# A gated state-space layer on one core: eight groups' scans rearranged around their small matrix products

## The chip, the core and the metric

The kernel runs on one core of a Trainium2 chip. The core has a matrix engine, TensorE (PE in the profile; PEld is its loading of weights), and three engines for elementwise work: VectorE (DVE), ScalarE (ACT) and GpSimd (POOL). SyncE (SP) issues the DMA transfers. Each engine takes its instructions in order and waits on semaphores where it needs another's result. PE writes to PSUM, eight banks of 512 float32 columns by 128 partitions; all other operands lie in SBUF. The metric is the time of one execution on the device in microseconds, the median of several runs.

## The reference

One layer of a hybrid decoder, for a prompt of 256 positions with 16 learned ones ahead of it, and for 8 samples of 8 positions each: 336 rows of 2048 channels.

```python
h = rms_norm(x, norm_w)
proj = h @ w_in
z, xbc, dt_raw, sc_b, sc_c, sc_h, sc_z, g_a, g_b = split_proj(proj)
...
xbc = jax.nn.silu(xbc_c + ssd_conv_b)
...
y_diag = jnp.einsum('bcijgr,bcjgrp->bcigrp', wts, xc)
...
chunk_states = jnp.einsum('bcjgr,bcjgrp,bcjgn->bcgrpn', to_end, xc, bc)
...
y_off = jnp.einsum('bcign,bcgrpn->bcigrp', cc, h_in) * jnp.exp(acum)[..., None]
...
y = gated_group_rms_norm(y.reshape(bsz, length, D_INNER), z, ssd_norm_w)
y_a = y @ w_ssd_out
...
merged = jax.nn.sigmoid(g_a) * y_a + jax.nn.sigmoid(g_b) * y_b
return x + merged @ w_o, conv_new, state, sconv_new
```

The scan is over chunks: within a chunk the outputs are weighted sums (`y_diag`), a state of 64 x 128 per head is carried from chunk to chunk, and what it contributes is `y_off`. The eight samples start from states of their own, which are inputs, and return new ones. The 64 heads fall into 8 groups of 8.

## The kernel before

All matrix products of the big weights are made in a split form: each float32 weight block is read by one DMA into `wraw`, ACT makes a rounded part `whi` (L86), DVE the rest `wlo` (L88), and PE multiplies `whi` with both parts of the activations (L94, L95) and `wlo` with the first (L98). A block is 128 x 1024; each of the three buffers has three copies. The type fp32r of these parts goes through PE in one instruction per product, a plain float32 product in two.

After a first stage (short convolution, gates, tables of the decay) comes the stage that the change touches: a loop over the 8 groups. For each group, four kinds of units follow one another, and each is a stretch of big products: `z_units` (4 units, the gate z of this group), `out_units` (8 units, the output projection of the group before, into `ya`), in the first and the last group `gate_units`, and `conv_units` (6 units, the inputs of the next group). Between the units the scan of the group, the generator `ssd`, is woven in: it is cut into steps by `yield`, and `weave` takes steps out so that 23 are done by the end of the units. Instructions of a step on PE, DVE and ACT are held behind the last L98, L88 and L86 traced before them; those of POOL and SP are not held. A planner orders what is free to move.

The steps, by their lines in `ssd`: `rows(c)` transposes a chunk's inputs and forms its products (two ms tiles); `decay` and `weights` make the matrices of weights W on DVE, ACT and POOL; `carry(c)` scales the state on POOL; `state(c)` (L496) forms a chunk's contribution to the state on PE in an ms tile and adds it, on DVE (L500), or copies it, on ACT, for the first chunk (L502). In the step of `state(1)` stand the carried outputs of the samples, `po` (L535 to L539): eight products with 32 columns of weights, four of them side by side in the array. One step later DVE takes them into `yo` (L543), and the shrinks (L506) begin: eight POOL instructions, two a step over four steps, which multiply the samples' states in place by their decay. Two steps after that come the weighted sums `yb` (L549 to L556), 32 float32 products on 64-column tiles, then four transposes of `yo` (L559) and the sums on DVE (L561 to L564). The states and inputs of the last chunk, which holds the meta positions and the samples, are split into parts and written to DRAM (L576, L577), read back in another order (L584 to L592), and used in `state(2)` with 64 rows (L604) and in the samples' states `up` with 32 rows (L610), added on DVE (L613). The gated result is squared on ACT (L581), summed over tiles on POOL (L594) and over channels on PE (L599); the factor r (L600 to L602) is spread over all partitions by a product of ones with a diagonal (L616 to L620).

PSUM holds two `pj` tiles (big products, one bank each), two `ms` tiles (one bank each) and one `yb` tile of four banks. `pj` is given back when the last reader has read it: for z these are ACT's tanh (L431) and DVE's product (L432).

Of the kernel before, what the change touches and what calls it, by code (L numbers as in the profile page):

```python
# [7 lines left out]
F32 = mybir.dt.float32  # L8
# [5 lines left out]
P = 128  # L14
# [20 lines left out]
def fb(ap):  # L35
    return ap.bitcast(F32)


def bc(ap, shape):
    return ap.to_broadcast(shape)  # L40
# [3 lines left out]
def tile_hybrid_step(ctx, tc, xT, w1, w2, wdt, wso, wsc, wo, cmask, vec, hvec, convst, sconvst, h0T,  # L44
# [330 lines left out]
    with tc.tile_pool(name="pb", bufs=2) as pb:  # L375
# [48 lines left out]
        def z_units(g, st):  # L424
            st["zs"] = []
            for t in range(4):
                pz = proj(w1[4 * g + t], META)
                z = pb.tile([P, TV + 4], F32, name="zs", bufs=4)
                if t == 0:
                    nc.gpsimd.memset(z[:, TV:], 0.0)  # L430
                nc.scalar.activation(z[:, :TV], pz, AF.Tanh, scale=0.5)  # L431
                nc.vector.scalar_tensor_tensor(z[:, :TV], z[:, :TV], 1.0, pz, add, mult)  # L432
                st["zs"].append(z)
                yield

# [6 lines left out]
        def ssd(g, st):  # L442
# [39 lines left out]
            def weights(c):  # L482
                n, m, w = CH[c][1], NT[c], W[c]
                nc.vector.tensor_tensor(w[:n], w[:n], bc(cbm[c][:n, :m].unsqueeze(1), [n, 8, m]), mult)
                xe[c] = big("xe", 2)
                nc.gpsimd.tensor_tensor(split(xe[c][:n]), split(xdt[c][:n]), bc(hv(tet[:n, c, :], g), [n, 8, HP]), mult)
                if c == 1:
                    nc.gpsimd.tensor_tensor(E, E, bc(CT[:, P:P + PX].unsqueeze(1), [P, 8, PX]), mult)

            def carry(c):  # L490
                hst[c] = hn = big("hst", 2)
                if c:
                    nc.gpsimd.tensor_tensor(split(hn), split(hst[c - 1]), bc(hv(cdec[:, c - 1, :], g), [P, 8, HP]),
                                            mult)

            def state(c, lhs, rhs):  # L496
                pst = ps.tile([P, 512], F32, name="ms")
                nc.tensor.matmul(pst, lhs, rhs, start=True, stop=True)  # L498
                if c:
                    nc.vector.tensor_tensor(hst[c], hst[c], pst, add)  # L500
                else:
                    nc.scalar.activation(hst[c], pst, AF.Copy)  # L502

            def shrink(b0, b1):
                for b in range(b0, b1):
                    nc.gpsimd.tensor_tensor(split(h0[b]), split(h0[b]), bc(hv(decS[:, b, :], g), [P, 8, HP]), mult)  # L506
# [25 lines left out]
            decay(2)  # L532
            yield
            state(1, bt[1], xe[1])
            po = ps.tile([P, 512], F32, name="ms")  # L535
            for s_ in range(2):
                for q in range(4):
                    nc.tensor.matmul(po[32 * q:32 * q + 32], CZ[:, 64 * q + 32 * s_:64 * q + 32 * s_ + 32],  # L538
                                     h0[2 * q + s_], start=s_ == 0, stop=s_ == 1)  # L539
            yield  # L540
            weights(2)
            yo = big("xe", 2)
            nc.vector.tensor_tensor(split(yo), split(po), bc(hv(eaY, g), [P, 8, HP]), mult)  # L543
            shrink(0, 2)
            yield
            carry(2)
            shrink(2, 4)
            yield
            yb = ps.tile([P, 4, 512], F32, name="yb", bufs=1)  # L549
            for t in range(4):  # L550
                for i, (x, w, t0, n) in enumerate(((xdt[0], W[0], 0, P), (xdt[1], W[1], P, PX), (hst[0], E, P, PX),
# [17 lines left out]
            nc.scalar.activation(bhh[:80, 0, :], bt[2][:80], AF.Copy)  # L569
            nc.vector.tensor_tensor(xe2[:80, 1, :], xe[2][:80], fb(xe2[:80, 0, :]), sub)  # L570
            nc.vector.tensor_tensor(bhh[:80, 1, :], bt[2][:80], fb(bhh[:80, 0, :]), sub)
            shrink(4, 6)
            yield
            xq, bq = xq_d[g % 2], bq_d[g % 2]
            for r in range(2):
# [3 lines left out]
            for t in range(4):  # L579
                nc.vector.tensor_tensor(ys[:, t, META:], ys[:, t, META:], zs[t][:, :TV], mult)  # L580
                nc.scalar.activation(zs[t][:, :TV], ys[:, t, META:], AF.Square)  # L581
            shrink(6, 8)
            yield
            x3 = big("xdt", 3, F32R)  # L584
            b3 = pb.tile([P, P], F32R, name="b3", bufs=1)
            xh = pb.tile([P, 2, 576], F32R, name="xh", tag="W")[:, :, :512]
            bh = pb.tile([P, 2, P], F32R, name="bh", bufs=1)
            for d, q in ((x3, xq), (b3, bq)):
                nc.sync.dma_start(fb(d[:64]), q[:16].rearrange("p r c -> (p r) c"))
            for d, q in ((xh, xq), (bh, bq)):  # L590
                for u in range(2):
                    nc.sync.dma_start(fb(d[:, u, :]), q[16 + 32 * u:48 + 32 * u].rearrange("p r c -> (p r) c"))  # L592
            for t in range(1, 4):
                nc.gpsimd.tensor_tensor(zs[0][:, :TV], zs[0][:, :TV], zs[t][:, :TV], add)  # L594
            yield
# [4 lines left out]
            r = pb.tile([107, 3], F32, name="rs_r", bufs=1)  # L600
            nc.vector.tensor_scalar(r, pr[:107, 0:3], 1.0 / 512, 4.0 * EPS, mult, add)
            nc.gpsimd.tensor_tensor(r, r, bc(mhalf[:107], [107, 3]), ALU.pow)  # L602
            yield
            state(2, b3[:64], x3[:64])  # L604
            nc.sync.dma_start(ssmp[g], hst[2])
            for u in range(2):
                up = ps.tile([P, 4, 512], F32, name="yb", bufs=1)
# [5 lines left out]
                    nc.vector.tensor_tensor(h, h, up[:, 2 * b:2 * b + 2, :], add)  # L613
                yield
                if u == 0:
                    dg = big("xe", 2)[:107, :321]  # L616
                    nc.vector.tensor_tensor(eights(dg, 107), bc(ident[:107, :107].unsqueeze(1), [107, 3, 107]),
                                            bc(r.unsqueeze(2), [107, 3, 107]), mult)
                    rs = ps.tile([P, 512], F32, name="ms")
                    nc.tensor.matmul(rs[:, :321], ones[:107, :], dg, start=True, stop=True)  # L620
                for b in range(2):
                    nc.sync.dma_start(ssms[g, :, 4 * u + 2 * b:4 * u + 2 * b + 2, :], h0t[2 * u + b])
                yield
# [237 lines left out]
```

## Time and profile before

| what | us |
|---|---|
| median of 3 runs | 1869.42 |
| lowest and highest | 1868.22, 1871.44 |
| the profiled execution, its own time | 1870.82 |
| its span | 1868.7 |
| DVE: weight rests L88, 480 of them | 604.2 busy, 1259 ns each |
| POOL: shrinks L506, 64 of them | 72.4 busy, 1167 ns each |
| DVE: samples' states L613, 32 of them | 38.7 busy, 1214 ns each |
| ACT: z's tanh L431, 32 of them | 13.8 busy, 431 ns each |
| DVE: z's product L432, 32 of them | 15.4 busy, 480 ns each |

How to read the views: a page gives the busy time of each engine, the span in 40 slices with the busy share of each in tenths, the chain of work that ended last, and groups of instructions by line, with the idle time before them and what ended it. A timeline has start and duration in us, engine, line, operation, output and inputs, the shape (for PE the rows and columns of the array in use, then rows and columns of the moving operand), and how many were merged. PE's products overlap, so a row's duration is longer than the distance to the next one's start; what a product costs PE is that distance. Each float32 product appears as two instructions. Times shown by the chain of waits are from the same execution. The granted clock of PE was full in nearly the whole span (mean 0.996).

### The profile page before, as it was taken

Reading aid. Unit: us, or ns where it says so; the run is one execution under the profiler, and the core shown is the slowest. Engines: PE = TensorE matmul, PEld = TensorE weight load, DVE = VectorE, ACT = ScalarE, POOL = GpSimd, SP = SyncE. Lnnn points to the kernel's source line nnn. Section 1 sums busy time; section 2 is a strip of 40 time slices with the busy share of each in tenths; the row PEclk is TensorE's granted clock in tenths of the full one; section 3 lists DMA queues with packets and bytes.
Section 4 is the critical chain, followed back from the end, with each engine's and each line's share of the span. In section 5 each row is a group of like instructions: output and inputs, shape, how many; then the busy total and the mean of one; then the engine's idle time right before and its main releaser. Section 6 shows DMA issues by size and latency. Waiting matters only on the chain.

```text
span 1868.7 us, 31432 instructions
## 1 busy us (share of the span) xinstructions
PE 1836.0 (98%) x12618; PEld 1792.8 (96%) x12618; DVE 1122.9 (60%) x1746; ACT 748.8 (40%) x1038; POOL 299.5 (16%) x395
## 2 busy tenths in 40 slices
PE   7999999999999999999999999999999999999996
PEld 7999999999999999999899999999999999999996
DVE  6844444454533335657577677876867677674533
ACT  6433333333333334445454353544435345333431
POOL 0100000000000001132221412214132231300011
PEclk9999999999999999999999999999999999999998
DMA  6444444444444446456466574655756466575553
GB/s 221 145 151 147 147 153 151 149 147 151 153 158 157 154 165 224 148 186 226 149 215 204 176 236 150 216 193 175 246 154 227 165 197 224 162 260 169 172 172 108
DMA packets 117185, 331.73 MB, mean 178 GB/s; under 512 B 12464, under 2 KB 38704, under 8 KB 117040
## 3 DMA queue, kind: packets, MB, share of 16 engines
q1 hardware_dynamic: 117040, 329.73, 53.9%
q8 instruction: 99, 1.62, 0.3%
q14 instruction: 46, 0.38, 0.1%
HBM read 296.80 MB, written 32.88 MB: 176 GB/s over the span
## 4 chain that ended last, share of the span: by engine, by line
PE 49%; DVE 1%; issue 1%; DMA 0%; ACT 0%; POOLq 0%; POOL 0%; DVEq 0%; ACTq 0%
PE pj L94 15%; PE pj L95 15%; PE pj L98 15%; PE yb L555 1%; PE ms L498 1%; PE ms L538 1%; DVE wlo L88 0%; PE ms L462 0%; DVE ya L754 0%; PE yb L610 0%; PE ms L559 0%; PE ms L465 0%; PE ms L620 0%; DMA wraw<-wso 0%; PE ms L599 0%
## 5 line engine op out<-in xcount | busy, mean ns | idle before, releaser
L88 DVE TENSOR_TENSOR wlo<-wraw,whi 128x1024 fp32r<-128x1024 f32 x480 | 604.2, 1259 | 490.6 <-ACT whi L86 244.4
L94 PE MATMUL pj<-hhi,whi 128*128 128x320 f32 (+3 forms) x2944 | 888.5, 313 | 0.0
L95 PE MATMUL pj<-hlo,whi 128*128 128x320 f32 (+3 forms) x2944 | 882.3, 312 | 0.0
L86 ACT ACTIVATE whi<-wraw 128x1024 fp32r<-128x1024 f32 x480 | 508.4, 1059 | 891.5 <-PE pj L95 753.9
L94 PEld LDWEIGHTS pj<-hhi,whi 128*128 128x128 f32 x2944 | 553.7, 188 | 5.4 <-issue 2.8
L95 PEld LDWEIGHTS pj<-hlo,whi 128*128 128x128 f32 x2944 | 553.0, 188 | 0.7
L98 PE MATMUL pj<-hhi,wlo 128*128 128x320 f32 (+3 forms) x2944 | 498.3, 311 | 0.0
L98 PEld LDWEIGHTS pj<-hhi,wlo 128*128 128x128 f32 x2944 | 453.2, 188 | 0.0
L94 PE MATMUL pj<-yh,whi 128*128 128x320 f32 x512 | 154.9, 314 | 4.3 <-DVE zs L432 2.5
L95 PE MATMUL pj<-yl,whi 128*128 128x320 f32 x512 | 152.7, 310 | 0.0
L94 PEld LDWEIGHTS pj<-yh,whi 128*128 128x128 f32 x512 | 96.0, 188 | 13.0 <-issue 6.4
L95 PEld LDWEIGHTS pj<-yl,whi 128*128 128x128 f32 x512 | 96.1, 188 | 0.0
L98 PE MATMUL pj<-yh,wlo 128*128 128x320 f32 x512 | 95.8, 308 | 0.0
L398 DVE SCALAR_TENSOR_TENSOR cacc<-pad,V,cacc 128x360 f32<-128x360 f32 (+1 forms) x144 | 89.6, 622 | 2.8
L647 DVE TENSOR_TENSOR ya<-ya,pj 128x320 f32<-128x320 f32 x112 | 54.1, 485 | 60.0 <-PE pj L98 59.5
L506 POOL TENSOR_TENSOR h<-h,decS 128x512 f32<-128x512 f32 x64 | 72.4, 1167 | 108.4 <-PE ms L538 94.4
L98 PEld LDWEIGHTS pj<-yh,wlo 128*128 128x128 f32 x512 | 80.3, 188 | 0.0
L197 POOL COPY SCS<-up 128x2 f32<-128x2 f32 x16 | 19.4, 1214 | 369.7 <-DVE up L191 366.7
L95 PE MATMUL pj<-vlo,whi 128*128 128x320 f32 x256 | 75.5, 309 | 0.0
L94 PE MATMUL pj<-vhi,whi 128*128 128x320 f32 x256 | 75.5, 309 | 0.0
L392 POOL COPY cs<-pad 128x3 f32<-128x3 f32 x48 | 42.4, 884 | 124.4 <-ACT pad L389 124.4
L95 PEld LDWEIGHTS pj<-vlo,whi 128*128 128x128 f32 x256 | 48.1, 188 | 0.0
(219 smaller groups left out, 1428.5 us busy)
## 6 DMA issues: line engine op xcount, KB each, us to landing
wraw<-w SPq DMA_DIRECT2D x352, 512.0 KB, 3.9
wraw<-wso SPq DMA_DIRECT2D x64, 512.0 KB, 3.5
wraw<-wsc SPq DMA_DIRECT2D x32, 512.0 KB, 3.8
h<-h0T SPq DMA_DIRECT2D x32, 512.0 KB, 5.7
ssms<-h SPq DMA_DIRECT2D x32, 512.0 KB, 5.7
wraw<-wo SPq DMA_DIRECT2D x32, 512.0 KB, 3.8
xq_d<-xe SPq DMA_DIRECT2D x16, 320.0 KB, 3.7
W<-ac_d SPq DMA_DIRECT2D x8, 576.0 KB, 6.7
```

Source lines behind the costliest of these rows:

```text
L86: latest["act"] = nc.scalar.activation(hi[:, :n], raw[:, :n], AF.Copy).ins
L88: latest["dve"] = nc.vector.tensor_tensor(lo[:, :n], raw[:, :n], fb(hi[:, :n]), sub).ins
L94: nc.tensor.matmul(out, w, xh(k0 + k), start=first and k == 0, stop=False)
L95: nc.tensor.matmul(out, w, xl(k0 + k), start=False, stop=False)
L98: latest["pe"] = nc.tensor.matmul(out, w, xh(k0 + k), start=False, stop=last and k == nk - 1).ins
L197: nc.gpsimd.tensor_copy(SCS[:, j, 0, :], up[:, 256:258])
L392: nc.gpsimd.tensor_copy(cs[:, 0, :], pad[:, 272:275])
L398: nc.vector.scalar_tensor_tensor(acc[:, i0:], pad[:, i0 + k:360 + k], col(V_CW, 4 * j + k), acc[:, i0:], mult, add)
L498: nc.tensor.matmul(pst, lhs, rhs, start=True, stop=True)
L506: nc.gpsimd.tensor_tensor(split(h0[b]), split(h0[b]), bc(hv(decS[:, b, :], g), [P, 8, HP]), mult)
L538: nc.tensor.matmul(po[32 * q:32 * q + 32], CZ[:, 64 * q + 32 * s_:64 * q + 32 * s_ + 32], h0[2 * q + s_], start=s_ == 0, stop=s_ == 1)
L647: nc.vector.tensor_tensor(ya[:, m, :TV], ya[:, m, :TV], pp[:, :TV], add)
```

## The change

Five edits in the scan and in `z_units`:

1. z: the tanh goes to a tile of its own (`cth`, one buffer, shared with the convolution); ACT also copies z out of `pj`, and DVE's product reads the two from SBUF.
2. `state(0)` and `state(1)` use the first bank of the `yb` tile instead of an `ms` tile.
3. The carried outputs `po` and `yo` move from the steps after `state(1)` into the step of the weighted sums, directly ahead of them; the shrinks move behind that step, three, three and two in the next three steps.
4. The prompt's last state multiplies all 128 rows; two POOL memsets clear rows 64 to 127 of its two operands.
5. The factor r is split into two fp32r parts on DVE, and spread by two fp32r products of 320 columns instead of one float32 product of 321.

```diff
@@ z_units
-                nc.scalar.activation(z[:, :TV], pz, AF.Tanh, scale=0.5)
-                nc.vector.scalar_tensor_tensor(z[:, :TV], z[:, :TV], 1.0, pz, add, mult)
+                th = pb.tile([P, 360], F32, name="cth", bufs=1)[:, :TV]
+                nc.scalar.activation(th, pz, AF.Tanh, scale=0.5)
+                nc.scalar.activation(z[:, :TV], pz, AF.Copy)
+                nc.vector.scalar_tensor_tensor(z[:, :TV], th, 1.0, z[:, :TV], add, mult)
@@ state
-                pst = ps.tile([P, 512], F32, name="ms")
+                pst = ps.tile([P, 512], F32, name="ms") if c == 2 else ps.tile([P, 4, 512], F32, name="yb", bufs=1)[:, 0]
@@ ssd, after state(1)
             state(1, bt[1], xe[1])
+            yield
+            weights(2)
+            yield
+            carry(2)
+            yield
             po = ps.tile([P, 512], F32, name="ms")
...
-            yield
-            weights(2)
             yo = big("xe", 2)
             nc.vector.tensor_tensor(split(yo), split(po), bc(hv(eaY, g), [P, 8, HP]), mult)
-            shrink(0, 2)
-            yield
-            carry(2)
-            shrink(2, 4)
-            yield
             yb = ps.tile([P, 4, 512], F32, name="yb", bufs=1)
@@ the next three steps
-            shrink(4, 6)
+            shrink(0, 3)
...
-            shrink(6, 8)
+            shrink(3, 6)
...
+            for d in (x3, b3):
+                nc.gpsimd.memset(fb(d[64:]), 0.0)
             for d, q in ((x3, xq), (b3, bq)):
                 nc.sync.dma_start(fb(d[:64]), q[:16].rearrange("p r c -> (p r) c"))
...
+            shrink(6, 8)
@@ after r
+            rh = pb.tile([107, 2, 3], F32R, name="rs_h", bufs=1)
+            nc.vector.tensor_copy(rh[:, 0, :], r)
+            nc.vector.tensor_tensor(rh[:, 1, :], r, fb(rh[:, 0, :]), sub)
...
-            state(2, b3[:64], x3[:64])
+            state(2, b3, x3)
@@ factor
-                    dg = big("xe", 2)[:107, :321]
-                    nc.vector.tensor_tensor(eights(dg, 107), bc(ident[:107, :107].unsqueeze(1), [107, 3, 107]),
-                                            bc(r.unsqueeze(2), [107, 3, 107]), mult)
                     rs = ps.tile([P, 512], F32, name="ms")
-                    nc.tensor.matmul(rs[:, :321], ones[:107, :], dg, start=True, stop=True)
+                    for i in range(2):
+                        dg = big("xe", 2, F32R)[:107, :321]
+                        nc.vector.tensor_tensor(eights(dg, 107), bc(ident[:107, :107].unsqueeze(1), [107, 3, 107]),
+                                                bc(fb(rh[:, i, :]).unsqueeze(2), [107, 3, 107]), mult)
+                        nc.tensor.matmul(rs[:, :TV], onesR[:107, :], dg[:, :TV], start=i == 0, stop=i == 1)
```

## The prediction

> **What bounds the kernel now.** I read the page first: the busy shares, the slices and the chain of work that ended last.
>
> ```profile
> span 1868.7 us, 31432 instructions
> ...
> PE 1836.0 (98%) x12618; PEld 1792.8 (96%) x12618; DVE 1122.9 (60%) x1746; ACT 748.8 (40%) x1038; POOL 299.5 (16%) x395
> ...
> PE   7999999999999999999999999999999999999996
> ...
> PE 49%; DVE 1%; issue 1%; DMA 0%; ACT 0%; POOLq 0%; POOL 0%; DVEq 0%; ACTq 0%
> ...
> L86 ACT ACTIVATE whi<-wraw 128x1024 fp32r<-128x1024 f32 x480 | 508.4, 1059 | 891.5 <-PE pj L95 753.9
> ```
>
> PE is busy in every slice and the chain names hardly anything else. The last row says that the engines that feed it are ahead: ACT stood idle 891.5 us before its weight conversions, 753.9 of them until PE gave a buffer back. So work added on ACT, DVE or POOL costs nothing until it uses up that lead; a saving must be PE time, either a wait of PE or an instruction on PE. The view of PE's waits lists the first kind, the chain in order of time shows how often the second comes.
>
> ```profile
> PE pj L94 <- DVE zs L432: 2.5, 3, 1.4
> PE ms L464 <- ACT hst L502: 1.6, 1, 1.6
> ```
>
> ```profile
> 1030.80 1.85 PE ms L538 x16
> ...
> 1145.44 1.85 PE ms L538 x16
> ```
>
> The scan of one group of heads comes round every 114.6 us, eight times in all. I work out one middle group (its state products of the samples, L538, at 1030.8) and multiply by eight.
>
> **The last state on all rows (L604).** PE's timeline in the two steps that add the samples' states: the first step also holds the prompt's last state (L498, 64 rows), the second doesn't.
>
> ```profile
> 1076.10 1.40 PE L98 MATMUL pj<-hhi,wlo 128*128 128x336 f32 x8
> 1077.43 0.50 PE L498 MATMUL ms<-xdt,b 64*128 64x512 f32 x1
> 1077.86 0.51 PE L610 MATMUL yb<-xh,bh 32*128 32x512 f32 x4
> ...
> 1078.56 0.32 PE L95 MATMUL pj<-hlo,whi 128*128 128x336 f32 x1
> ...
> 1092.55 1.40 PE L98 MATMUL pj<-hhi,wlo 128*128 128x336 f32 x8
> 1093.88 0.51 PE L610 MATMUL yb<-xh,bh 32*128 32x512 f32 x4
> ...
> 1094.57 0.31 PE L95 MATMUL pj<-hlo,whi 128*128 128x320 f32 x1
> ```
>
> From the L98 row to the L95 row it is 2.46 us with L498 and 2.02 without, so the 64-row product takes 0.44 us of PE. The same product over the whole array should cost what its columns cost. The rows of the next step give that price:
>
> ```profile
> 1084.59 1.40 PE L98 MATMUL pj<-hhi,wlo 128*128 128x336 f32 x8
> 1085.83 0.70 PE L620 MATMUL ms<-xe,CR 107*128 107x321 f32 x2
> ...
> 1086.52 0.32 PE L95 MATMUL pj<-hlo,whi 128*128 128x336 f32 x1
> ```
>
> Eight full-array products of 336 columns take 1.24 us, 0.155 each; 512 columns make 0.236. The step from the full array to the 32-row products stays, and is in the 2.02 already. Saved: 0.44 - 0.236 = 0.20, times eight **1.6 us** (1.4 to 1.8). The two memsets that fill rows 64 to 127 are POOL's; I bound each by one shrink (1.13 us, below) and cost them at nothing, since L498 comes some 30 us after the last reader of that buffer. If SP's load of the lower rows had to wait for the memset, the weight loads behind it on SP would wait too, on a lead of about two blocks.
>
> **The factor in two parts (L616 to L620).** By the same rows, from L620 to the L95 after it are 0.69 us, less one ordinary 0.155: 0.535 us for a float32 product of 321 columns, which runs as two instructions. The new form is two fp32r products of 320 columns, 0.148 each by the row above, 0.295 together. Saved 0.24, times eight **1.9 us** (1.5 to 2.1). What DVE gets instead:
>
> ```profile
> 1075.52 0.49 DVE L617 TENSOR_TENSOR xe<-CR,rs_r 107x321 f32<-107x321 f32 x1
> ```
>
> That is one more diagonal of 0.49 us and two tiny splits, each below that: under 1.5 us per group. DVE had the diagonal ready at 1076.0, PE used it at 1085.83; the cover is ten us, and what would be late without it is L620 itself, by at most the 1.5. The second diagonal takes the buffer of yo, whose last reader is L559, long done.
>
> **The carried outputs beside the weighted sums (L535 to L543 moved behind carry(2)).** Rows of the two places that become one, and DVE's evacuation from the listing of groups by shape:
>
> ```profile
> 1029.78 1.02 PE L498 MATMUL ms<-xe,bt 128*128 128x512 f32 x2
> 1030.73 1.92 PE L538 MATMUL ms<-h,CZ 128*32 128x512 f32 x16
> ...
> 1032.84 0.31 PE L95 MATMUL pj<-yl,whi 128*128 128x320 f32 x1
> ...
> 1042.66 0.75 PE L98 MATMUL pj<-yh,wlo 128*128 128x320 f32 x4
> 1043.34 0.68 PE L555 MATMUL yb<-W,xdt 128*64 128x128 f32 x8
> ...
> 1046.89 0.66 PE L559 MATMUL ms<-CR,xe 128*128 128x128 f32 x4
> ```
>
> ```profile
> L543 DVE TENSOR_TENSOR xe<-ms,eaY 128x512 f32<-128x512 f32 x8 | 5.5, 692 | 4.4 <-PE ms L538 4.4
> ```
>
> One float32 pass costs 0.268 for 321 columns (half of 0.535), so 0.427 for 512. L498 to L538 is 0.95, two passes and 0.10 for going to 32-column tiles. L538 to the L95 is 2.11: less four rounds of four tiles side by side (1.71) and one ordinary 0.147, that leaves 0.25 for going back. L98 to L555 is 0.68, four products of 0.147 and 0.09 for going to 64 columns. Of these 0.44 us the change keeps one entry (0.10), and has a step from 32 to 64 columns that no row shows. Its ends: nothing, and the 0.20 over its columns that L498 shows going from 64 to 32 rows; below nothing is excluded, a switch gives no time back. I take 0.14, nearest to the two measured entries to column tiles with their slower first product. Saved 0.44 - 0.10 - 0.14 = 0.20, times eight **1.6 us** (1.1 to 2.7). The Trainium skill, TensorEngine Tiling (Array Packing), Key Properties, says that changing the tiling mode drains the engine, not a mere change of tile. By it the end at nothing falls away, and 2.0 would be the most.
>
> New is a wait: yo must leave ms on DVE before the transposes L559, in the same step. PE has the weighted sums to do in between, 1046.89 - 1043.34 = 3.55 us, against 0.69 for yo, so 2.8 us are left for whatever stands before yo on DVE. Queued behind yo are the evacuations of yb, which must wait for the sums anyway, and the next wlo. The shrinks move with it (they overwrite what L538 reads) and are off PE; see the slower rival.
>
> **z by ScalarE (L431, L432).** One of the three waits, in DVE's, ACT's and PE's timelines:
>
> ```profile
> 1125.10 1.21 DVE L88 TENSOR_TENSOR wlo<-wraw,whi 128x1024 fp32r<-128x1024 f32 x1
> 1126.23 0.47 DVE L432 SCALAR_TENSOR_TENSOR zs<-zs,pj 128x320 f32<-128x320 f32 x1
> ```
>
> ```profile
> 1124.40 0.44 ACT L431 ACTIVATE zs<-pj 128x320 f32<-128x320 f32 x1
> ```
>
> ```profile
> 1126.76 0.41 PE L94 MATMUL pj<-yh,whi 128*128 128x320 f32 x1 [0.63 <-DVE zs L432]
> ```
>
> ACT had read pj at 1124.84, but DVE's part came behind a wlo and let go at 1126.70, and PE waited. With the copy on ACT, of the same length as the tanh, pj is free at about 1125.3, before PE asks for it at 1126.1. All three waits go: **2.5 us** (0 to 2.8; the lower end if the planner puts a whi of 1.06 us between tanh and copy where it hurts). Late next would be the weights, which have their lead. ACT pays 32 x 0.44 = 14 us, hidden at a share of 40%. The new tanh tile has one buffer, shared with the convolution's; its reader on DVE comes within two us, the next tanh some seven later.
>
> **States in the four-bank tile (L497).** The last group's wait, on ACT and in the chain:
>
> ```profile
> 1583.76 0.41 ACT L431 ACTIVATE zs<-pj 128x320 f32<-128x320 f32 x1
> 1584.08 0.58 ACT L502 ACTIVATE hst<-ms 128x512 f32<-128x512 f32 x1
> ```
>
> ```profile
> 1584.71 0.31 PE ms L464
> ...
> 1586.09 0.59 PE pj L98 x4
> ```
>
> PE's transposes wanted the ms buffer that state(0) held until ACT's copy. With that state in yb, whose four banks stand empty then, the buffer is free. PE would run 1.6 us earlier and want z's pj at 1586.68 - 1.6 = 1585.1; that is free at 1584.17 + 0.44 = 1584.6, so little is given back: **1.5 us** (0 to 1.6).
>
> **Sum:** 1.6 + 1.9 + 1.6 + 2.5 + 1.5 = 9.1 us. The profiled execution took 1870.82 us, 2.1 of them around its span, and gives 1861.7; it lies 1.40 above the median of the runs shown, 1869.42, from which I get **1860.3**.
>
> **Rivals.** *The waits come back*: z's copy stands behind other ACT work and the last group waits for z instead. Then 4.0 us go and 5.1 stay: 1864.3. For it speaks that ACT issues in order; against it, that ACT was free when PE waited. *yo is late*: three wlo of 1.21 stand before yo on DVE and need 3.6 us where 2.8 are free, and PE waits at L559 for 0.8 us per group, 6.6 in all: 1866.9, no change that can be measured. Against it: DVE stood waiting for the sums in this step already. *The order doesn't come out*: other products are put between L538 and L555, and that term is lost: 1861.9.
>
> *Slower*: POOL becomes late for the square sums that PE waits for at L599.
>
> ```profile
> 1031.86 9.04 POOL L506 TENSOR_TENSOR h<-h,decS 128x512 f32<-128x512 f32 x8 [13.98 <-PE ms L538]
> ```
>
> ```profile
> 1036.91 2.08 DVE L88 TENSOR_TENSOR wlo<-wraw,whi 128x1024 fp32r<-128x1024 f32 x1
> ```
>
> ```profile
> 1047.00:1070.00 23.00, 23.00 (x155) 23.00 (x156) 16.66 (x27) 11.89 (x21) 8.04 (x14) 1.00 0.71 221
> ```
>
> ```profile
> 1069.34 0.64 PE L599 MATMUL ms<-CR,zs 128*107 128x1 f32 x6
> ```
>
> If the eight shrinks (9.04) fall wholly behind the sums, POOL has 8.04 + 9.04 + 2.3 for memsets = 19.4 us of work in the 22.3 until L599 (the fourth to sixth figures of the window are DVE, ACT, POOL busy). DVE is busy 16.66 there, and beside shrinks a wlo took 2.08 where it took 1.21 elsewhere. Were half of DVE's time, 8.3, pushed onto POOL, L599 would be 5.4 us late, 43 in all: 1903. It costs from 2.9 us on, and turns the change slower from about 4.5. The Trainium skill, SBUF — State Buffer, section SBUF: two separate sides, has DVE and GpSimd exclude each other on a shared port pair for a whole instruction; the 2.08 agrees, and moving z's second operand out of PSUM gives DVE one more such instruction. Against the rival: the shrinks were written into four steps and ran as one block as soon as L538 was through, so they would start near 1045.
>
> **How the numbers follow.** Forecast 0.62, waits back 0.20, order 0.03, yo late 0.10, POOL 0.05. The best ends (1.8, 2.1, 2.7, 2.8, 1.6) make 11.0 and 1858.4; the worst (1.4, 1.5, 1.1, 0, 0) 4.0 and 1865.4. The three runs lie from 1.2 below to 2.0 above their median, so the range is 1856.5 to 1866.5, which holds the first three cases and leaves yo and POOL out. 0.2%, or 3.7 us, is about what a measurement of this kernel can tell from no change: faster 0.86, same 0.09, slower 0.05.
>
> **What would show it.** From L98 to the L95 after state(2) and L610 2.26 us instead of 2.46; the factor's two products 0.15 us each instead of 0.27; L538 straight before L555, with 0.14 us between them beyond the columns; no L432 or L502 among PE's waits. A wait of PE on yo, on POOL's zs or on ACT's copy, longer weight conversions on PE's chain, or a span above 1866, would prove me wrong.

## The result, and the profile after

The changed kernel took 1857.58 us, the median of 4 runs (1855.04 to 1859.89), beside 1869.93 (1868.22 to 1871.44, 4 runs) for the kernel before in the same comparison: a ratio of 0.9935 with a 95% interval of 0.9922 to 0.9947. That is 12.3 us less; 9.1 had been forecast, and the forecast of 1860.3 lies 2.7 us above the time. A second, later comparison (below) gave 1858.35 against 1866.39, a ratio of 0.9953 (0.9940 to 0.9967), 8.0 us. So the kernel is faster by 8 to 12 us, and the two comparisons differ by 4.3. Much of the work below is about that difference.

The page of the kernel after, from its busy times, its chain and its groups:

```profile
span 1856.0 us, 31512 instructions
...
PE 1828.3 (99%) x12618; PEld 1792.8 (97%) x12618; DVE 1133.9 (61%) x1770; ACT 757.7 (41%) x1070; POOL 318.1 (17%) x411
...
PE 67%; DVE 1%; issue 1%; DMA 0%; ACT 0%; POOLq 0%; POOL 0%; DVEq 0%; ACTq 0%
...
L86 ACT ACTIVATE whi<-wraw 128x1024 fp32r<-128x1024 f32 x480 | 508.7, 1060 | 861.8 <-PE pj L95 746.0
```

PE's busy time fell by 7.7 us (1836.0 before) and its idle time in the span by 5.0 (span less busy: 32.7 before, 27.7 after). DVE, ACT and POOL have 9 to 19 us more work each and nothing came of it: ACT still stands idle 746.0 us for PE to give a buffer back. PE remains the bound.

Where PE's time went is read from the distance between the starts of neighbouring products, since their rows overlap. The lines of the kernel after are shifted: the states' products are L500, po L545, the weighted sums L555, the transposes of yo L559, the samples' states L616, the factor L627. A middle group of the kernel after, three places in PE's timeline:

```profile
1036.24 0.75 PE L98 MATMUL pj<-yh,wlo 128*128 128x320 f32 x4
1036.92 1.92 PE L545 MATMUL ms<-h,CZ 128*32 128x512 f32 x16
1038.77 0.68 PE L555 MATMUL yb<-W,xdt 128*64 128x128 f32 x8
...
1042.32 0.65 PE L559 MATMUL ms<-CR,xe 128*128 128x128 f32 x4
...
1071.53 1.40 PE L98 MATMUL pj<-hhi,wlo 128*128 128x336 f32 x8
1072.77 0.40 PE L500 MATMUL ms<-xdt,b 128*128 128x512 f32 x1
...
1073.80 0.31 PE L95 MATMUL pj<-hlo,whi 128*128 128x336 f32 x1
...
1081.05 0.46 PE L627 MATMUL ms<-xe,CR 107*128 107x320 f32 x2
...
1081.51 0.31 PE L95 MATMUL pj<-hlo,whi 128*128 128x336 f32 x1
```

L98 to L95 around the last state is 2.27 us (2.46 before). L627 to L95 is 0.46, less one ordinary product of 0.155 leaves 0.305 for the factor (0.535 before). From L545 to L555 it is 1.85: four rounds of 0.427 and 0.14 for the step from 32 to 64 columns. L559 follows 3.55 us after L555, exactly as before, so the transposes didn't wait for yo.

A fourth place had not been in the forecast: `state(0)` and the transposes of the last chunk, `rows(2)`. PE's timeline before:

```profile
1013.39 0.75 PE L98 MATMUL pj<-yh,wlo 128*128 128x320 f32 x4
...
1014.84 0.60 PE L462 MATMUL ms<-CR,xs 128*80 128x128 f32 x4
1015.19 0.39 PE L94 MATMUL pj<-yh,whi 128*128 128x320 f32 x1
...
1015.81 0.31 PE L464 MATMUL ms<-CR,BT 128*80 128x128 f32 x1
...
1016.29 0.31 PE L94 MATMUL pj<-yh,whi 128*128 128x320 f32 x1
```

and after:

```profile
1009.15 0.75 PE L98 MATMUL pj<-yh,wlo 128*128 128x320 f32 x4
...
1010.60 0.60 PE L464 MATMUL ms<-CR,xs 128*80 128x128 f32 x4
1011.03 0.27 PE L466 MATMUL ms<-CR,BT 128*80 128x128 f32 x1
...
1011.47 0.31 PE L95 MATMUL pj<-yl,whi 128*128 128x320 f32 x1
```

Before, state(0) held one ms tile until ACT had copied it, the second ms tile of rows(2) was not yet free, and the planner put three big products into the gap (1015.19 to 1015.81). PE lost no time waiting, but broke its stream of big products twice. From the first row to the last it is 2.90 us, less three products of 0.147, 2.46; after, 2.32 in one go. The second break had cost 0.14 us per group.

And the step in which PE asks for the bank of z, before and after:

```profile
1011.30 0.75 PE L98 MATMUL pj<-yh,wlo 128*128 128x320 f32 x4
...
1012.36 0.31 PE L95 MATMUL pj<-yl,whi 128*128 128x320 f32 x1
```

```profile
1007.39 0.75 PE L98 MATMUL pj<-yh,wlo 128*128 128x320 f32 x4
...
1008.12 0.31 PE L95 MATMUL pj<-yl,whi 128*128 128x320 f32 x1
```

It is 1.06 us before and 0.73 after, and 0.73 is what five products of 0.147 make. DVE's timeline before shows what PE waited for:

```profile
1011.59 0.47 DVE L432 SCALAR_TENSOR_TENSOR zs<-zs,pj 128x320 f32<-128x320 f32 x1
```

DVE let go of the bank at 1012.06; PE's next product began at 1012.11. The view of waits doesn't list this one: rows of PE last 0.3 us where products follow each other by 0.147, so a stop below some 0.3 us leaves little or no gap between rows.

One wait came back. In the last group, PE, and ACT at the same time:

```profile
1575.59 0.41 PE L94 MATMUL pj<-yh,whi 128*128 128x320 f32 x1 [1.06 <-ACT zs L433]
```

```profile
1574.16 0.74 ACT L482 ACTIVATE W<-W 80x640 f32<-80x640 f32 x1 [3.00 <-DVE W L480]
1574.80 0.42 ACT L432 ACTIVATE cth<-pj 128x320 f32<-128x320 f32 x1
1575.12 0.42 ACT L433 ACTIVATE zs<-pj 128x320 f32<-128x320 f32 x1
```

The decay's exponential stood ahead of z's tanh on ACT and itself waited 3.00 us for DVE.

What each place gave in the first pair of traces, in us over the eight groups, each the sum of start-to-start distances less the big products between:

| place on PE | before | after | gain |
|---|---|---|---|
| state(2) and the step into the 32-row products | 9.01 | 7.59 | 1.4 |
| factor | 4.35 | 2.43 | 1.9 |
| state(1), po and the weighted sums with transposes | 56.34 | 54.75 | 1.6 |
| state(0) and rows(2), without waits | 13.8 | 12.7 | 1.1 |
| z's bank, groups 1 to 6 | 4.07 | 0 | 4.1 |
| last group: ms bank | 1.69 | 0 | 1.7 |
| last group: z's bank | 0 | 1.33 | -1.3 |
| `ya`, last group and end | 2.12 | 0.93 | 1.2 |
| around the loop | | | 0.8 |

Together these are the 12.5 us by which PE's time from first to last product fell.

### The profile page after: what moved, and what is told of

It reads as the page before. It is cut to its first block, busy times and chain, and to the rows that moved or that the text cites. A ratio compares the mean times of both kernels' runs of the same rounds, so it can differ in the third digit from the quotient of the medians.

```text
span 1856.0 us, 31512 instructions
## 1 busy us (share of the span) xinstructions
PE 1828.3 (99%) x12618; PEld 1792.8 (97%) x12618; DVE 1133.9 (61%) x1770; ACT 757.7 (41%) x1070; POOL 318.1 (17%) x411
## 4 chain that ended last, share of the span: by engine, by line
PE 67%; DVE 1%; issue 1%; DMA 0%; ACT 0%; POOLq 0%; POOL 0%; DVEq 0%; ACTq 0%
PE pj L94 21%; PE pj L95 20%; PE pj L98 20%; PE yb L555 2%; PE ms L545 1%; PE yb L500 1%; PE ms L464 1%; DVE ya L761 0%; PE yb L616 0%; DVE wlo L88 0%; PE ms L467 0%; PE ms L559 0%; PE ms L602 0%; DMA h<-mb_d 0%; DMA wraw<-wso 0%
## 5 line engine op out<-in xcount | busy, mean ns | idle before, releaser
L95 PE MATMUL pj<-hlo,whi 128*128 128x320 f32 (+3 forms) x2944 | 882.2, 312 | 0.0
L88 DVE TENSOR_TENSOR wlo<-wraw,whi 128x1024 fp32r<-128x1024 f32 x480 | 596.7, 1243 | 462.0 <-PE pj L98 235.8
L86 ACT ACTIVATE whi<-wraw 128x1024 fp32r<-128x1024 f32 x480 | 508.7, 1060 | 861.8 <-PE pj L95 746.0
L95 PEld LDWEIGHTS pj<-hlo,whi 128*128 128x128 f32 x2944 | 553.0, 188 | 0.3 <-issue 0.2
L98 PE MATMUL pj<-hhi,wlo 128*128 128x320 f32 (+3 forms) x2944 | 498.4, 311 | 0.0
L98 PEld LDWEIGHTS pj<-hhi,wlo 128*128 128x128 f32 x2944 | 453.2, 188 | 0.0
L95 PE MATMUL pj<-yl,whi 128*128 128x320 f32 x512 | 152.2, 309 | 0.0
L95 PEld LDWEIGHTS pj<-yl,whi 128*128 128x128 f32 x512 | 96.3, 188 | 1.7 <-issue 1.7
L98 PE MATMUL pj<-yh,wlo 128*128 128x320 f32 x512 | 95.9, 309 | 0.0
L98 PEld LDWEIGHTS pj<-yh,wlo 128*128 128x128 f32 x512 | 80.4, 188 | 0.0
L95 PE MATMUL pj<-vlo,whi 128*128 128x320 f32 x256 | 75.5, 309 | 0.0
L391 POOL COPY pad<-cs 128x24 f32<-128x24 f32 x48 | 33.6, 702 | 114.3 <-DVE cacc L398 93.0
```

The source lines that it names most:

```text
L86: latest["act"] = nc.scalar.activation(hi[:, :n], raw[:, :n], AF.Copy).ins
L88: latest["dve"] = nc.vector.tensor_tensor(lo[:, :n], raw[:, :n], fb(hi[:, :n]), sub).ins
L95: nc.tensor.matmul(out, w, xl(k0 + k), start=False, stop=False)
L98: latest["pe"] = nc.tensor.matmul(out, w, xh(k0 + k), start=False, stop=last and k == nk - 1).ins
L391: nc.gpsimd.tensor_copy(smp[:, :, 0:3], cs[:, 1:9, :])
```

## The experiments

Unless something else is said, each edit is made to the changed kernel. Single executions of one kernel scatter: the kernel before gave 1863.66 to 1871.44 over all its runs, up to 4.5 us from the median of their comparison, so single times can't tell 1 us apart. The runs also come from several chips: e1 to e4 stand beside 1863.66 for the kernel before and e5 to e8 beside 1867.60 (one execution each), e9 to e12 beside a median of 1866.39 (9 runs). The distances on PE can: where nothing is waited for, they are the same to 0.01 us in every trace. Beside them I use one stretch, from the first transposes of the first group to the last product of the samples' states, the "eight groups" below.

| run | time, us | eight groups, us |
|---|---|---|
| before | 1869.93 (4 runs) | 886.03 |
| after | 1857.58 (4 runs) | 874.42 |
| e1_z_dve | 1858.49 | 874.93 |
| e2_states_ms | 1858.59 | 875.38 |
| e3_rows64 | 1858.99 | 875.46 |
| e4_factor_f32 | 1858.58 | 875.05 |
| e5_po_early | 1859.53 | 875.63 |
| e6_po_shrinks_early | 1857.95 | 875.64 |
| e7_hold_exp | 1855.51 | 873.11 |
| e8_sums_f32r | 1859.03 | 870.96 |
| e9_before_again | 1864.69 | 883.37 |
| e10_z_and_states | 1860.77 | 876.48 |
| e11_after_again | 1858.35 (5 runs) | 873.14 |
| e12_best | 1855.68 (5 runs) | 871.99 |

### e1_z_dve: z's second operand from PSUM on DVE again

```diff
-                th = pb.tile([P, 360], F32, name="cth", bufs=1)[:, :TV]
-                nc.scalar.activation(th, pz, AF.Tanh, scale=0.5)
-                nc.scalar.activation(z[:, :TV], pz, AF.Copy)
-                nc.vector.scalar_tensor_tensor(z[:, :TV], th, 1.0, z[:, :TV], add, mult)
+                nc.scalar.activation(z[:, :TV], pz, AF.Tanh, scale=0.5)
+                nc.vector.scalar_tensor_tensor(z[:, :TV], z[:, :TV], 1.0, pz, add, mult)
```

> The changed kernel with only the z edit undone: DVE reads z from pj again. Theory (the distances between PE's products): in groups 1 to 6 the step from the last L98 of the first output tile to the first L94 of the second is back at 0.3 to 1.7 us instead of 0.15, six waits of about 4.1 us in all with the slower first product behind each; the last group's wait of 1.2 us there stays or grows; the profiled execution takes 1861.5 to 1863 instead of 1858.0. Rival (the view of waits as it stands): only three waits come back, 2.5 us in all, and the step is ordinary in the other groups: 1860.5.

PE's timeline in the middle group:

```profile
1008.94 0.75 PE L98 MATMUL pj<-yh,wlo 128*128 128x320 f32 x4
...
1009.96 0.31 PE L95 MATMUL pj<-yl,whi 128*128 128x320 f32 x1
```

1.02 us where the changed kernel has 0.73: 0.28 lost, in each of groups 1 to 5, and 0.38 in group 6, together 1.8. The long waits of the kernel before, three in its view of waits with 2.5 us, did not come back, and neither theory's number fits. What the z edit removes in every execution is six short steps that the view doesn't list; the long ones are something else. The last group's wait for z was also gone.

### e2_states_ms: all states in ms again

```diff
-                pst = ps.tile([P, 512], F32, name="ms") if c == 2 else ps.tile([P, 4, 512], F32, name="yb", bufs=1)[:, 0]
+                pst = ps.tile([P, 512], F32, name="ms")
```

> The changed kernel with only the bank of the first two states undone: they take an ms tile again. Theory: the transposes and products of the third chunk are cut in two by big products in every group, and a second break costs PE 0.13 us per group, 1.1 in all; the last group waits 1.7 us for ACT's copy of the state again, and its wait of 1.3 for z goes: 1859.5 instead of 1858.0. Rival: a second break costs nothing, so only the last group differs, by 0.4: 1858.4.

The second break is back, with the distances of the kernel before (state(0) and rows(2) together 1.72 us per group in place of 1.59), so it belongs to this edit: 1.1 us over the loop. The last group's wait is back as well, in the view of PE's waits:

```profile
PE ms L466 <- ACT hst L504: 1.1, 1, 1.1
```

### e3_rows64 and e4_factor_f32: the two instruction terms

```diff
-            for d in (x3, b3):
-                nc.gpsimd.memset(fb(d[64:]), 0.0)
...
-            state(2, b3, x3)
+            state(2, b3[:64], x3[:64])
```

> The changed kernel with only the rows of the prompt's last state undone: 64 rows, no memsets. Theory: from the L98 before it to the L95 after it PE takes 0.19 us more than the 0.88 (less two ordinary products) of the changed kernel, in every group, 1.5 in all: 1859.5. Rival: a product costs by its columns whatever its rows, and the difference of the two kernels came from elsewhere: 0.88 stays, 1858.0.

```diff
-            rh = pb.tile([107, 2, 3], F32R, name="rs_h", bufs=1)
...
-                    for i in range(2):
-                        dg = big("xe", 2, F32R)[:107, :321]
...
-                        nc.tensor.matmul(rs[:, :TV], onesR[:107, :], dg[:, :TV], start=i == 0, stop=i == 1)
+                    dg = big("xe", 2)[:107, :321]
...
+                    nc.tensor.matmul(rs[:, :321], ones[:107, :], dg, start=True, stop=True)
```

> The changed kernel with only the factor undone: one float32 product of 321 columns, one diagonal on DVE. Theory: PE takes 0.54 us for it instead of 0.31, 1.9 in all: 1859.9. Rival: DVE, with a diagonal and two splits fewer per group, lets PE's remaining waits go, and no more than half of the 1.9 shows: 1859.

PE's timelines, first e3, then e4:

```profile
1072.79 1.40 PE L98 MATMUL pj<-hhi,wlo 128*128 128x336 f32 x8
...
1075.25 0.32 PE L95 MATMUL pj<-hlo,whi 128*128 128x336 f32 x1
```

```profile
1081.29 0.70 PE L623 MATMUL ms<-xe,CR 107*128 107x321 f32 x2
...
1081.99 0.32 PE L95 MATMUL pj<-hlo,whi 128*128 128x336 f32 x1
```

2.46 and 0.70 us: the distances of the kernel before, to 0.01. Over the loop the first costs 1.42, the second 1.92. Both terms stand as they were worked out. In e3 PE also waited once, 0.6 us, for a square on ACT, which is in no other trace.

### e5_po_early and e6_po_shrinks_early: the carried outputs back at their place

e5 puts po behind state(1) and yo behind weights(2), and leaves the shrinks where the change has them; e6 writes the shrinks into the old steps too.

```diff
             state(1, bt[1], xe[1])
+            po = ps.tile([P, 512], F32, name="ms")
...
             yield
             weights(2)
+            yo = big("xe", 2)
+            nc.vector.tensor_tensor(split(yo), split(po), bc(hv(eaY, g), [P, 8, HP]), mult)
             yield
             carry(2)
             yield
-            po = ps.tile([P, 512], F32, name="ms")
...
```

> The changed kernel with the samples' carried outputs back behind state(1) and their evacuation one step later, but the shrinks left where the change put them. Theory: the three changes of tiling instead of two cost PE 0.19 us per group, 1.5 in all, and nothing else moves: 1859.5 instead of 1858.0. Rival: what the move gave was DVE's relief from the shrinks, so nothing is lost here: 1858.

> As the run before, with the shrinks in their old steps too. Theory: the same 1.5 us on PE, and in the last group the shrinks lie beside DVE's weight rests again: one of these takes about 2.1 us instead of 1.2, and PE waits 0.9 us for an evacuation of the output projection that the changed kernel and the run before do not wait for: 1860.4. Rival: that wait is scatter of one execution, and the two runs are alike: 1859.5.

On PE both give 0.20 us per group back, 1.6 over the loop, as forecast. And both show a wait in the last group that the changed kernel hasn't. It is not scatter: PE's timeline has it in all four traces with po in its early place (0.70 in the kernel before and again in e9, 0.69 and 0.70 here) and in none of the ten others. The row of e5 and that of e6:

```profile
1596.58 0.39 PE L94 MATMUL pj<-yh,whi 128*128 128x320 f32 x1 [0.69 <-DVE ya L654]
```

```profile
1594.51 0.39 PE L94 MATMUL pj<-yh,whi 128*128 128x320 f32 x1 [0.70 <-DVE ya L655]
```

e6 was to tell whether the place of the shrinks makes it. The two are alike (875.63 and 875.64), so the place in the code doesn't; POOL's timelines, again e5 and then e6, say why they had to be alike:

```profile
1587.85 9.09 POOL L508 TENSOR_TENSOR h<-h,decS 128x512 f32<-128x512 f32 x8 [9.49 <-PE ms L540]
```

```profile
1585.78 9.10 POOL L508 TENSOR_TENSOR h<-h,decS 128x512 f32<-128x512 f32 x8 [9.27 <-PE ms L540]
```

POOL isn't held by steps. In both kernels the eight shrinks ran as one block as soon as po had read the first of the states. DVE worked beside that block, in e5:

```profile
1592.91 2.08 DVE L88 TENSOR_TENSOR wlo<-wraw,whi 128x1024 fp32r<-128x1024 f32 x1
1594.91 1.13 DVE L571 TENSOR_TENSOR bhh<-bt,bhh 80x128 fp32r<-80x128 f32 x1
```

and where po comes late (e11, the changed kernel), the same two instructions:

```profile
1589.06 1.23 DVE L88 TENSOR_TENSOR wlo<-wraw,whi 128x1024 fp32r<-128x1024 f32 x1
1590.20 0.28 DVE L571 TENSOR_TENSOR bhh<-bt,bhh 80x128 fp32r<-80x128 f32 x1
```

Beside the shrinks the pair took 3.21 us, without them 1.51. Behind it on DVE stands the evacuation of ya that PE waits for, 1.7 us later than it would be. With po late the block begins just ahead of the weighted sums (1596.62 and 1597.35 in e11) and runs beside them, when DVE has to wait for PE's sums anyway. The rows show this chain; a kernel with po early and the shrinks kept away from it, which would test it alone, was not run.

### e7_hold_exp: the exponential behind z's copy

ACT's exponential of the decay is held behind the copy of z, so that it can't stand ahead of the tanh; the order changes in the last group only.

```diff
-                nc.scalar.activation(z[:, :TV], pz, AF.Copy)
+                st["zc"] = nc.scalar.activation(z[:, :TV], pz, AF.Copy).ins
@@ out_units
-                hi, lo = wblk(wso[g, mp])
+                hi, lo = wblk(wso[g, mp]); latest["z"] = S[min(g + 1, NG - 1)]["zc"]
```

> The changed kernel with one order added: the exponent of the last chunk's decay may not pass ahead of z's copy on ACT (only the last group is ordered otherwise). Theory: the last group's wait of 1.2 us for z, and the slower product behind it, go; nothing is late next: 1856.6 instead of 1858.0. Rival: the wait turns into one for the state's copy or the decay behind it, and the sum stays: 1858.

The wait was gone and the eight groups took 873.11, 1.31 less, as the theory had it. That looked like a proof until the changed kernel was traced again (e11): there the wait didn't occur either, and the eight groups took 873.14. The edit does no harm; that it gains anything isn't shown.

### e8_sums_f32r: the square sums in fp32r

The sums of squares over channels (L602) take six float32 instructions of one column. Here POOL writes its last sum rounded to fp32r, and three products of two columns follow; so r is computed from rounded squares.

```diff
+            zq = big("xe", 2, F32R)[:, :TV + 4]
...
-                nc.gpsimd.tensor_tensor(zs[0][:, :TV], zs[0][:, :TV], zs[t][:, :TV], add)
+                nc.gpsimd.tensor_tensor(zq[:, :TV] if t == 3 else zs[0][:, :TV], zs[0][:, :TV], zs[t][:, :TV], add)
...
-                nc.tensor.matmul(pr[:107, c:c + 1], zs[0][:, 107 * c:107 * c + 107], ones[:, 0:1], start=True, stop=True)
+                nc.tensor.matmul(pr[:107, 2 * c:2 * c + 2], zq[:, 107 * c:107 * c + 107], onesR[:, 0:2], start=True, stop=True)
```

> The changed kernel with the sums of squares over channels in one part: POOL's last addition writes them rounded to fp32r, and three fp32r products of two columns take the place of three float32 products of one column (two instructions each). Theory: each instruction costs its load of weights, 0.094 us, so three fewer save 0.28 per group, 2.2 us in all: 1855.7. Rival: an fp32r product of two columns takes as long as the pair it replaces: 1858.

PE's timelines of a middle group, in e11 and then in e8:

```profile
1065.53 0.64 PE L602 MATMUL ms<-CR,zs 128*107 128x1 f32 x6
1066.03 0.40 PE L94 MATMUL pj<-hhi,whi 128*128 128x336 f32 x1
```

```profile
1065.24 0.35 PE L604 MATMUL ms<-CR,xe 128*107 128x2 f32 x3
1065.46 0.40 PE L94 MATMUL pj<-hhi,whi 128*128 128x336 f32 x1
```

The sums hold PE for 0.22 us in place of 0.50, and the eight groups took 870.96, 2.2 less than in e11. The time, 1859.03, shows nothing of it. It is lost at the end, in the view of PE's waits:

```profile
PE pj L94 <- DVE ya L656: 3.3, 1, 3.3
```

In e11 this wait was 0.35. The rest, by which the work behind the eight groups grew (209.36 us in place of 205.08), is the clock; see e12.

### e9_before_again and e11_after_again: how much is scatter

The kernels before and after without any edit, in the later comparison.

> The kernel before once more, for a second trace. Theory: the short steps of 0.28 us for z in groups 1 to 6 belong to the order and come again, while the long waits there (1.53, 0.80 and 0.65 in groups 1, 3 and 4) follow weight loads that come late, because SP's queue stands on the store of the samples' states ahead of them, and differ from execution to execution. Rival: the planned order sets the long ones too: the same groups within 0.1 us.

PE's waits of the kernel before in this execution:

```profile
PE ms L464 <- ACT hst L502: 0.9, 1, 0.9
...
PE pj L94 <- DVE zs L432: 0.6, 1, 0.6
```

2.5 us in three waits for z have become 0.6 in one, and in another group. The short steps are there as before: 0.28 us in each of groups 1 to 5. The last group's wait for the ms bank is 0.9, not 1.6. So the short steps belong to the kernel, and the long ones to the execution. The eight groups took 883.37, 2.7 less than in the first trace of the same kernel.

> The changed kernel once more. Theory: the last group's wait of 1.2 us for z is one of order and comes again within 0.3; the eight groups take 874.4 us on PE within 0.7; the median lies between 1855.5 and 1859. Rival: the wait is scatter and goes to below 0.3: 873.1.

The rival was right: the last group's wait for z, 1.06 in the first trace, didn't occur, and the eight groups took 873.14, 1.3 less than in the first trace.

More of the scatter lies where the change doesn't reach. From PE's first product to the first transposes of the first group, the same code in all kernels, it is 753.5 us in e9 and 754.7 in e6, 755.4 to 756.5 in ten traces, and 757.2 in e3 and e5. Some 40 us into the span the granted clock stays at 1.00 in e9 and e6, is at 0.50 for 3.4 us in the ten, and for 6.8 in e3 and e5; a wait of PE for DVE in the same place lasts from 0.7 us (e9) to 2.2 (e2). Windows of e9 and of the first trace of the kernel before; the granted clock is the third figure from the end:

```profile
40.00:43.00 3.00, 3.00 (x22) 3.00 (x22) 3.00 (x6) 1.16 (x3) 0.00 (x0) 1.00 0.22 74
```

```profile
40.00:43.00 3.00, 3.00 (x15) 2.90 (x16) 1.51 (x4) 0.45 (x1) 0.00 (x0) 0.64 0.01 5
```

Of the 6.1 us between these two executions, 2.7 lie in this stretch and 2.7 in the eight groups. The times of other executions go with their mean granted clock as well: in the later comparison the kernel before took 1864.22 to 1866.39 at 0.996, 1867.80 to 1868.05 at 0.995 and 1870.85 at 0.994. So the eight groups tell more of the change than the times do: they gained 11.6 us in the first pair of traces and 10.2 in the second (883.37 to 873.14), whose executions differ by only 7.8.

### e10_z_and_states: both PSUM edits undone

The edits of e1 and e2 together, to see whether the long waits need both.

> The changed kernel with both the z edit and the states' bank undone. Theory: the two are worth what each is worth alone; groups 1 to 6 show the step of 0.28 us for z, 1.7 in all, every group the second break, 1.1, and the last group a wait for the state's copy of 1.1 to 1.7 in place of 1.3 for z; the eight groups take 877.0 to 877.8 us on PE instead of 874.4. Rival: only the two together keep ACT and DVE behind, and the long waits for z are back, 2.4 us more: 879.5 or above.

876.48, 0.5 below the theory's lowest number and 3.0 below the rival's. The second break was back in full, the z steps were 0.28 in four groups and 0.47 and 0.53 in two, and the last group's wait for the ms bank was about 0.15 only. The two edits add up: 3.3 us more than e11, 2.1 of them for z and 1.2 for the second break with the short wait. The long waits don't come with them.

### e12_best: both further edits together

e7 and e8 in one kernel.

> The changed kernel with the exponent held behind z's copy and the sums of squares in one fp32r part. Theory: 1.3 us of the last group's wait and 2.2 us of sums go, the eight groups take 870.9 us, and PE's wait of 3.3 us for an evacuation at the end, seen once with the fp32r sums, was a slow transfer of that execution: 3.5 us below the changed kernel of the same call. Rival: the order of the end of the kernel is what made it wait, it comes again, and the two are level.

1855.68 us, a ratio of 0.9942 (0.9928 to 0.9956) to the kernel before; e11 in the same comparison 0.9953 (0.9940 to 0.9967). The median is 2.7 us lower, but the intervals overlap, so it is not shown to be better than the change alone. The eight groups took 871.99, 1.0 more than in e8, all of it in the last group: PE waited there for ACT's tanh of a gate and, 0.6 us between starts, for the two diagonals of the factor on DVE (listed as 0.2). These were late in no other trace, but in the last group they are never far ahead: the second was ready 1.9 us before PE used it in the changed kernel (first trace) and 0.3 in e8.

Three views show what holds it: PE's waits, SP's waits near the end, and windows (PE, PEld, DVE, ACT and POOL busy, then PE's granted clock, DMA share and GB/s).

```profile
PE pj L94 <- DVE ya L656: 2.0, 2, 1.8
```

```profile
SPq L675 <- DMA ssms<-h: 5.6, 3, 3.3
```

```profile
1648.00:1650.00 2.00, 0.86 (x6) 0.59 (x5) 2.00 (x4) 1.06 (x1) 0.00 (x0) 1.00 0.89 266
...
1653.00:1654.00 1.00, 1.00 (x6) 1.00 (x5) 0.35 (x1) 0.00 (x0) 0.00 (x0) 0.50 1.12 390
```

At the end of the loop SP waits for the stores of the samples' states before it can load into the same buffers what the merge needs; DVE waits for those loads, ya stays in its bank, and PE waits. PE reaches this place one to two us earlier (the eight groups) and waits longer: 1.80 in e12 and 3.29 in e8, where e11 has 0.35. That is more than it came earlier: counted from the first transposes of the first group, the bank also came free 0.6 (e12) and 0.9 us (e8) later than in e11; why is open. The granted clock, 1.00 in the first window, is at half in the second, just after the wait: PE worked all of it at half its rate, from about 1651.4 to 1654.8. The same happened behind the wait of e8. So what the sums gave on PE was lost to a longer wait and a slower clock behind it, and the stores of the samples' states are the next thing to move.

## Why the prediction was right

The forecast was right in sign, in the bound and in its range; its sum of 9.1 us was 3 us less than the gain of the first comparison and 1 more than that of the second. The 12.3 us exceed even the 11.0 to which its best ends add up; the time is in the range only by what was allowed for scatter. By its own steps:

- **What bounds the kernel**: PE, and work added elsewhere costs nothing. Held: no longer weight conversions on the chain, and DVE's and POOL's additions hidden in the changed kernel. ACT's were late for PE once, in the first of its two traces (below).
- **The last state on all rows**, 1.6 (1.4 to 1.8): 1.42, shown by e3: 0.19 in a middle group, where 0.20 was worked out, and less than half of that in the last group.
- **The factor in two parts**, 1.9: 1.92, shown by e4. The cover of ten us was that of a middle group; in the last group the one diagonal of the kernel before was 3.8 us ahead of PE, and the second of the changed kernel 1.9.
- **The carried outputs**, 1.6: 1.6, shown by e5. The step from 32 to 64 columns, which no row of the kernel before had, cost 0.14 beyond the columns, the value taken. By the Trainium skill, TensorEngine Tiling (Array Packing), Key Properties, a change of tiling mode drains the engine; the 0.14 agrees, and the end at nothing is out. A gain of the same move that was not forecast: the last group's wait for ya, 0.9 us with the slower first pair of products behind it, is gone; by the rows of e5 and e11 because the shrinks no longer run beside DVE's work there, which no run tests alone.
- **z by ScalarE**, 2.5: the step that failed in kind. The view of waits gave three long waits, and these were taken for the whole and for something that comes every time. Together with the short ones they gave 4.1 in the first pair of traces, but e1 and e9 show that the long ones differ from execution to execution; what recurs is 0.28 us in six groups, 1.7 to 1.8 in all, hidden in the overlap of PE's rows. That the size came out near 2.5 was luck. In the group where PE waits at 1126.76 DVE worked without a break from 1119.48 to 1126.70; in e9 it stood idle twice for over 1 us, for ACT's weights, just before the same step. So DVE had fallen behind in the first trace; what put it behind is open.
- **States in the four-bank tile**, 1.5: the wait that was read from the chain was 1.7 on PE in the first trace and about 1.0 in e9. Mis-sized by leaving out that the same bank had split rows(2) in two: 1.1 us over the loop, as sure as the instruction terms, and shown by e2. It could have been read from PE's timeline before, where three big products stand between L462 and L464.

The terms that come every time are 1.4 + 1.9 + 1.6 + 1.1 + 1.7 + 0.9 = 8.6 us, and the last group's wait for the ms bank added 0.9 or more in both traces of the kernel before. That this lies so near 9.1 is luck in part: 0.8 too much for z and 0.5 for the bank stand against 2.0 that were not forecast, the second break and the wait for ya. The two comparisons gave 8.0 and 12.3; the waits that change from execution to execution, up to 2.4 us for z and 1.3 given back in the last group, are as large as that difference, and so is what the stretch ahead of the loop varies by, 753.5 to 757.2. Which of them made it isn't shown, since only one execution of each was traced.

The rivals: *waits come back* happened in one of the changed kernel's two traces, in the last group as described, and cost 1.3, not the whole of the two terms; a wait on ACT's copy was one of the prediction's own signs of being wrong. None of the six edited kernels that keep z's lines (e2 to e6, e8) shows it. *yo is late* did not: L559 follows the sums at the old distance. *The order doesn't come out* did not: L545 stands straight before L555. *Slower, POOL late*: no wait of PE for the square sums is in any of the traces. The slowing it was built on is real and the Trainium skill, SBUF — State Buffer, section SBUF: two separate sides, which has DVE and GpSimd exclude each other on a shared port pair, agrees with 2.08 us for a wlo beside the shrinks and 1.23 without. But it worked for the change: the block of shrinks moved from under DVE's weight work to under the weighted sums.

## What to carry to other kernels

Where PE is the bound, count its time by distances between starts and over every group, for stops of a few tenths leave no idle time in the view of waits, and a bank that is late can show as a split stream and no wait at all. Trace the kernel before twice before a long wait is taken for a gain: what recurs is worth its full price, what differs from execution to execution isn't. Where whole executions scatter by more than the gain, compare the stretch that the change touches. And an engine that isn't held by program order, as POOL here, runs its work when its input allows; to move a collision, move the producer it waits for, not its line in the code.

## What the runs showed of the hardware

- Breaking the stream of big products a second time, with no wait in it, costs 0.14 us.
- A 64-row product cost 0.44 us of PE, and the same product with its rows filled up to 128, half of them zeros, 0.25.
- DVE's small instruction of 80 x 128 went from 0.28 to 1.13 us beside POOL's shrinks, the wlo from 1.23 to 2.08. The factors differ widely, but both took 0.85 us more, somewhat less than one shrink (9.09 us for eight). A row doesn't tell which part of its time is waiting.
- A wait of PE can cost more than its length. Behind 1.80 us (e12) and 3.29 us (e8) the granted clock went to 0.50 for some 3.4 us, with big products 0.27 us apart where they are 0.147 otherwise, a loss of about 1.5 us each time; behind 1.39 us (e10) it stayed at 1.00. No length of wait follows from this: near 40 us into the span the clock went to 0.50 behind waits of 1.05 and 0.69 us in e7, and stayed at 1.00 behind 1.92 and 0.70 in e6. The Trainium skill, TensorE: Matmul & The Clock Gate, Part 1, has a gate that halves the clock after an idle window of about 3.4 us and opens it after a busy one as long. The half and the 3.4 us agree; the waits of e12 and e7 are shorter than the page's idle window, and here the measurement decides.
